# Splitting the next layer's weights earlier, a two-step low part, and tile addresses at multiples of 64 bytes

## The chip, the cores and the metric

The kernel runs on one NeuronCore of a Trainium2 chip. The metric is device time in microseconds (us) of the whole program; lower is better. TensorE (PE) multiplies, VectorE (DVE), ScalarE (ACT) and GpSimd (POOL) do elementwise work, SyncE (SP) issues all DMAs. Each engine works through its own instructions in order and waits for others by semaphores.

## The reference, cut to what matters

Two blocks of two layers each, on 512 tokens of width 1024 (and 256 context tokens in the first layer), all in float32:

```python
def reference(x, c, ctx, ...):
    x = first_block(x, c, ctx, ...)      # layer 0: window attention + short convolution; layer 1: HGRN2 scan
    return second_block(x, ...)          # an even and an odd mixer, each followed by a SwiGLU

def ab_layer(x, xc, mod, mod_c, w_in, w_out, ...):
    q, k, v, g_a, xb, b_g, c_g, g_b = split_cols(modulate(x, shift, scale) @ w_in, widths)
    ...
    y = jnp.concatenate([o_a * jax.nn.silu(g_a), o_b * jax.nn.silu(g_b)], axis=-1) @ w_out
    x_new = layer_norm(DEEPNORM_ALPHA * x + gate * y, ln_g, ln_b)

def second_block(x, ...):
    for layer in range(DEPTH):
        hn = rms_norm(x, norm_mix_pre[layer])
        mix = even_mixer(hn, ...) if layer % 2 == 0 else odd_mixer(hn, ...)
        x = x + rms_norm(mix, norm_mix_post[layer])
        hn = rms_norm(x, norm_ffn_pre[layer])
        ff = swiglu(hn, ffn_w_gate[layer], ffn_w_up[layer], ffn_w_down[layer])
        x = x + rms_norm(ff, norm_ffn_post[layer])
    return x
```

Every `@` here is a matrix product of the tokens with a weight matrix; those products are most of the work.

## The kernel before, in words

Activations stay transposed: a tile holds 128 features by up to 768 tokens, eight tiles make the width of 1024. A float32 product is made of three matmuls in the faster type fp32r: weights and inputs are each split into a high part (rounded to fp32r) and a low part (what the rounding left), and `product` (L293) adds high x high, high x low and low x high for each of eight tiles k. The names of a tile end in `_h` and `_l` for the two parts. In the profile's rows `mm<-act_h,wp_l` is a matmul into a bank of PSUM called mm, with the input tile act_h and the weight tile wp_l.

Weights come in blocks of 128 output columns, 512 KB each. `weights` (L269) loads a block into `wp_r` (3 buffers), rounds it to `wp_h` on ScalarE (`copy`, L243) and subtracts into `wp_l` (`sub`, L258) on VectorE, or on the engine given as `eng`. `wp_h` and `wp_l` have 4 buffers each, used in turn.

The stages run one after another: layer 0, layer 1, even, feed-forward 0, odd, feed-forward 1. A stage ends with `out_products` (L344): eight output blocks, the first ones over all tokens (512 columns per matmul), the last `keep` (3) by halves of 256 tokens (`PARTS`), so that the first half can be finished while the second is multiplied. These last blocks have their own buffers for `spare[1]` of them (pools w0, w5, w6, w7 or H). For each product `use` adds it to the running sums (res or po_mx or g_ff, and the sum of squares po_a or n_a). For each half `done` multiplies that sum with a matrix of ones (the matmul z, after which all partitions hold the mean), makes a reciprocal root, and then for each of the eight tiles k normalises, adds to the residual x and calls `emit` or `pre`, which write the next stage's inputs. `done` is a generator whose steps are interleaved with the second half's products.

`prenorm` (L1050) gives that `pre` for four boundaries (layer 1 to even, even to feed-forward 0, feed-forward 0 to odd, odd to feed-forward 1; the last stage has none): h is x times the norm's weight on ScalarE (`pn_h`), `act_h` its rounded copy on ScalarE, `act_l` the difference on GpSimd. `stats` then sums the squares of x into `res_acc`, and `rms` (L1079) turns it into the scale `res_rr` by a matmul with ones. At the boundary from layer 0 to layer 1 `emit` (L521) writes layer 1's inputs a_h and a_l, the subtraction in turns on VectorE and GpSimd.

The next stage begins with `firsts` (L304): three weight blocks, their low parts on GpSimd, are multiplied together tile by tile, first with the first half of the tokens, then with the second, so that each tile k is used as soon as it is there.

Three things set the order of work. Each engine's order is fixed when the program is built: a scheduler walks the instructions with priorities in the order in which the code emits them, and places one as soon as it reckons that it is ready. So a load or a split that the code emits late can still be placed early, where its buffers are free. The buffers' turns set the earliest time. And SP's order of DMAs is fixed in the same way.

Tiles lie in pools that are stacked from the left side of each partition's memory (const, wp, cond, a0, ...) or from the right (`side="right"`: a1, b2, b3, y1, z8, ...). A tile takes its width rounded up to 32 bytes.

Of the kernel before, what the change touches and what calls it, by code (L numbers as in the profile page):

```python
# [18 lines left out]
L = 512  # L19
# [169 lines left out]
class Prog:  # L189
    def __init__(self, es, tc, I, off):  # L190
# [21 lines left out]
        for v in (1e-5, 1e-6, np.pi / 2):  # L212
            t = self.const.tile([128, 1], F32, name=f"eps{int(v * 1e7)}")
            nc.gpsimd.memset(t, v)
            self.bias[v] = t
        self.rope2 = self.const.tile([128, 4], F32, name="rope2")
        nc.sync.dma_start(out=self.rope2, in_=I["rope2"])
        self.dummy = self.const.tile([128, 1], F32, name="dummy")

# [84 lines left out]
    def firsts(self, ps, blocks, xs, tags=("mm",) * 3):  # L304


        ws = [self.weights(b, eng=self.nc.gpsimd) for b in blocks]
        out = [ps(t) for t in tags]
        for s in PARTS[:2]:
            for k in range(KT):  # L310
                for p, w in zip(out[:3], ws):
                    self.product(p[:, s], w, xs, s, ks=(k,))
            for p, w in zip(out[3:], ws[3:]):
                self.product(p[:, s], w, xs, s)
        return list(zip(out, ws))
# [27 lines left out]

    def out_products(self, ps, block, xs, parts, use, done, keep=3, n=1024, late=(), begun=None, spare=(None, 0)):  # L344

# [19 lines left out]
        pool, own = spare  # L365
        ws = [self.weights(block(8 - keep + j), n, pool=pool if j < own else None) for j in range(keep)]
        last = iter(())
        for i, s in enumerate(parts):
# [27 lines left out]
    def conditioning(self, es):  # L396
# [12 lines left out]
        self.nc.vector.tensor_copy(out=self.sc[:, :, 0:2], in_=tv)  # L409
        self.sel = cond.tile([128, 2], F32, name="sel")  # L410
        self.nc.sync.dma_start(out=self.sel, in_=self.I["sel"])
# [41 lines left out]
    def layer0(self, stop=False):  # L453

        nc, tc = self.nc, self.tc
        with ExitStack() as es:
# [77 lines left out]
            use, done = self.deepnorm(N, ps, res, mod, emit)  # L534
            self.out_products(ps, lambda m: self.I["wo_ab"][m], xs2, PARTS, use, done, spare=(Alloc(es, tc, "w0", {"h": (1, 1024), "l": (1, 1024)}), 1))

# [281 lines left out]
    def layer1(self):  # L818
        nc, tc = self.nc, self.tc
        with ExitStack() as es:  # L820
# [23 lines left out]
            use, done = self.deepnorm(N, ps, self.x, self.mods[1], emit)  # L844
            self.out_products(ps, lambda m: self.I["wo_c"][m], xs2, PARTS[:2], use, done, spare=(Alloc(es, tc, "w5", {"h": (1, 1024), "l": (1, 1024)}), 1))
            for k in range(KT):
# [203 lines left out]
    def prenorm(self, es, ps, name, l):  # L1050


        nc = self.nc
        N = Alloc(es, self.tc, "pn", {"sq": (3, L), "h": (3, 256)})
        g = self.vec(name, 8 * l, 8 * l + 8)
        self.xs = [self.parts_of(self.A) for k in range(KT)]
        self.rr, self.acc = self.R("rr"), self.R("acc")

        def pre(k, s, x=None, scale=g, bias=None):
            hi, lo = self.xs[k]  # L1060
            h = N("h")
            x = self.x[k][:, s] if x is None else x
            if bias is None:
                self.act(h, x, ACT.Copy, scale=scale[:, k:k + 1])
            else:
                self.act(h, x, ACT.Identity, scale=scale[:, k:k + 1], bias=bias[:, k:k + 1])
            self.copy(hi[:, s], h)
            self.sub(lo[:, s], h, hi[:, s].bitcast(F32), nc.gpsimd)

        def stats():  # L1070
            for j in range(KT):
                sq = N("sq") if j else self.acc
                self.act(sq, self.x[j], ACT.Square)
                if j:
                    self.add(self.acc, self.acc, sq)

        return pre, stats
# [338 lines left out]
    def even(self):  # L1416
        tc = self.tc
        with ExitStack() as es:
# [5 lines left out]
            use, done = self.postnorm(es, ps, "norm_mix_post", 0, pre)  # L1424
            self.out_products(ps, lambda m: self.I["wo_ev"][m], xs2, PARTS[:2], use, done, late=(4, 5), begun=begun, spare=(Alloc(es, tc, "w6", {"h": (2, 1024), "l": (2, 1024)}), 2))
            stats()
# [212 lines left out]
    def odd(self):  # L1639
        tc = self.tc  # L1640
        with ExitStack() as es:
# [5 lines left out]
            use, done = self.postnorm(es, ps, "norm_mix_post", 1, pre)  # L1647
            self.out_products(ps, lambda m: self.I["wo_od"][m], xs2, PARTS[:2], use, done, late=(2, 4), spare=(Alloc(es, tc, "w7", {"h": (3, 1024), "l": (3, 1024)}), 3))
            stats()

    def odd_mix(self, es, B):
        nc, tc, xs, r = self.nc, self.tc, self.xs, self.rr
        A = Alloc(es, tc, "o7", {
            "sp2": (1, 8), "hb": (1, 16), "h": (4, L), "l": (4, L), "xb": (2, L + 3), "xc": (2, 1024),
            "tr": (2, 1024), "ti": (2, 1024), "a": (2, L), "mu": (2, L), "u": (2, 1024), "z": (2, 1024),
# [3 lines left out]
        sp = self.sp  # L1659
        sp2, hb = A("sp2"), A("hb")  # L1660
        self.ts(sp2, sp, 2.0, ALU.mult)
# [77 lines left out]
        halves, whole = (slice(0, L), slice(L, 2 * L)), (slice(0, 2 * L),)  # L1739
        first = dict(enumerate(self.firsts(ps, self.od[:3], xs)))  # L1740
        self.rms(ps("g"))
        cs, zs = {0: conv(0), 1: conv(1)}, {}
# [29 lines left out]
    def ffn(self, l, last=None):  # L1772

        nc, tc, xs, r = self.nc, self.tc, self.xs, self.rr
        with ExitStack() as es:
# [16 lines left out]
            for a, b in ((0, 6), (6, 14), (14, 22)):  # L1792
# [30 lines left out]
                else:  # L1823
# [4 lines left out]
                    use, done = self.postnorm(es, ps, "norm_ffn_post", l, pre, ff, last)  # L1828
                    self.out_products(ps, block, hs, PARTS[:2], use, done, n=n, keep=4 if last else 3, spare=(H, 2))
                    if stats:  # L1830
# [64 lines left out]
```

## Time and profile before

| | |
|---|---|
| three runs | 2106.44, 2109.29, 2116.51 us, median 2109.29 |
| profiled execution | 2109.53 us, of which the span is 2107.7 us |
| granted TensorE clock, mean | 0.986 of full speed |
| TensorE (matmuls) busy | 2038.4 us, 97% |
| VectorE, ScalarE, GpSimd busy | 1335.0, 918.5, 382.4 us |

Rows of the trace give a start in us from the span's start, a length, the engine, the line of the kernel, the operation, `output<-inputs`, the shape, and the number of instructions merged into the row; in brackets the idle time of the engine before it and what ended it. Matmuls overlap by their pipeline, so a matmul's own length (0.39 us) says less than the distance of two starts.

### The profile page before, as it was taken

How to read it: one execution, taken by the hardware profiler on the slowest of the kernel's cores; microseconds unless marked ns; L12 is line 12 of the kernel's file. 1: busy time of each engine (PE TensorE's matmuls, PEld its weight loads, DVE VectorE, ACT ScalarE, POOL GpSimd, SP SyncE). 2: the span in 40 equal slices, each digit the busy share in tenths (PEclk: the TensorE clock that was granted, in tenths of full speed). 3: DMA queues.
4: the chain of work that ended last, by engine and by line, in shares of the span. 5: the costliest groups of instructions: out<-in, count | busy, mean ns of one | idle time of the engine just before them, and what ended most of it. 6: DMA issues, size and time to landing. Idle time of an engine off the chain costs nothing. (4 is left out here: it accounts for less than half of the span.)

```text
span 2107.7 us, 30001 instructions
## 1 busy us (share of the span) xinstructions
PE 2038.4 (97%) x11624; PEld 1736.8 (82%) x11624; DVE 1335.0 (63%) x2302; ACT 918.5 (44%) x1642; POOL 382.4 (18%) x383
## 2 busy tenths in 40 slices
PE   6999999999999999989999999999989999999997
PEld 4888888889888888878778888888887888888886
DVE  6775566786666666787765764544567786344455
ACT  2564334445444444446566554322346654322231
POOL 1111111344222222033111420100020131010011
PEclk9999999999999999999999999999999999999998
DMA  8344442322111111224332398532325322333231
GB/s 307 117 155 138 148 137 73 116 82 77 42 52 57 53 51 41 90 96 146 115 100 81 132 325 321 170 100 91 121 98 201 130 90 88 103 100 100 91 109 41
DMA packets 91662, 246.91 MB, mean 117 GB/s; under 512 B 20480, under 2 KB 29440, under 8 KB 91520
## 3 DMA queue, kind: packets, MB, share of 16 engines
q1 hardware_dynamic: 91520, 245.01, 34.9%
q8 instruction: 91, 1.49, 0.3%
q14 instruction: 51, 0.42, 0.1%
HBM read 209.84 MB, written 35.13 MB: 116 GB/s over the span
## 5 line engine op out<-in xcount | busy, mean ns | idle before, releaser
L244 ACT ACTIVATE wp_h<-wp_r 128x1024 fp32r<-128x1024 f32 (+2 forms) x243 | 250.9, 1037 | 409.9 <-PE mm L318 245.8
L250 DVE TENSOR_TENSOR wp_l<-wp_r,wp_h 128x1024 fp32r<-128x1024 f32 (+1 forms) x228 | 319.6, 1404 | 100.2 <-ACT wp_h L244 100.1
L318 PE MATMUL mm<-act_l,wp_h 128*128 128x512 f32 (+1 forms) x1008 | 380.0, 377 | 2.6 <-POOL act_l L250 2.6
L318 PE MATMUL mm<-act_h,wp_h 128*128 128x512 f32 (+1 forms) x1008 | 377.5, 375 | 2.5 <-ACT act_h L244 2.5
L318 PE MATMUL mm<-act_h,wp_l 128*128 128x512 f32 (+1 forms) x1008 | 377.8, 375 | 0.0
L318 PE MATMUL mm<-a_h,wp_h 128*128 128x512 f32 (+1 forms) x920 | 337.1, 368 | 5.2 <-ACT wp_h L244 3.2
L318 PE MATMUL mm<-a_h,wp_l 128*128 128x512 f32 (+1 forms) x920 | 330.5, 360 | 0.4 <-POOL wp_l L250 0.4
L318 PE MATMUL mm<-a_l,wp_h 128*128 128x512 f32 (+1 forms) x920 | 329.3, 358 | 0.7 <-DVE a_l L250 0.6
L318 PEld LDWEIGHTS mm<-act_l,wp_h 128*128 128x128 f32 x1008 | 193.4, 192 | 36.4 <-POOL act_l L250 3.3
L318 PEld LDWEIGHTS mm<-act_h,wp_h 128*128 128x128 f32 x1008 | 192.3, 191 | 35.3 <-ACT act_h L244 2.9
L318 PEld LDWEIGHTS mm<-act_h,wp_l 128*128 128x128 f32 x1008 | 193.2, 192 | 33.0 <-issue 1.0
L318 PEld LDWEIGHTS mm<-a_h,wp_h 128*128 128x128 f32 x920 | 174.4, 190 | 30.2 <-issue 3.6
L318 PEld LDWEIGHTS mm<-a_l,wp_h 128*128 128x128 f32 x920 | 174.5, 190 | 25.9 <-issue 2.3
L318 PEld LDWEIGHTS mm<-a_h,wp_l 128*128 128x128 f32 x920 | 174.3, 189 | 24.0 <-issue 0.7
L250 POOL TENSOR_TENSOR g_g<-g_g,g_u 128x512 f32<-128x512 f32 x44 | 61.3, 1395 | 551.7 <-DVE g_u L250 510.0
L318 PE MATMUL mm<-h_l,wp_h 128*128 128x512 f32 (+1 forms) x344 | 129.2, 376 | 0.6 <-DVE h_l L250 0.5
L318 PE MATMUL mm<-h_h,wp_h 128*128 128x512 f32 (+1 forms) x344 | 129.0, 375 | 0.5 <-ACT h_h L244 0.5
L318 PE MATMUL mm<-h_h,wp_l 128*128 128x512 f32 (+1 forms) x344 | 128.8, 374 | 0.0
L250 DVE TENSOR_TENSOR g_u<-mm,res_rr 128x512 f32<-128x512 f32 x44 | 30.3, 689 | 110.6 <-PE mm L318 110.6
L244 ACT ACTIVATE m_km<-m_k 128x512 f32<-128x512 f32 x56 | 37.6, 672 | 122.9 <-DVE m_k L250 101.4
L247 ACT ACT_TABLE_LOAD x60 | 77.0, 1283 | 1.8 <-PEq L1883 0.7
L318 PEld LDWEIGHTS mm<-h_l,wp_h 128*128 128x128 f32 x344 | 64.8, 188 | 13.5 <-DVE h_l L250 2.1
(498 smaller groups left out, 3898.1 us busy)
## 6 DMA issues: line engine op xcount, KB each, us to landing
wp_r<-w_gu SPq DMA_DIRECT2D x88, 512.0 KB, 3.5
wp_r<-w_c SPq DMA_DIRECT2D x40, 512.0 KB, 3.5
wp_r<-wada SPq DMA_DIRECT2D x32, 512.0 KB, 3.7
wp_r<-w_d SPq DMA_DIRECT2D x32, 512.0 KB, 3.5
wp_r<-w_ab SPq DMA_DIRECT2D x26, 512.0 KB, 4.7
od_d<-z_h SPq DMA_DIRECT2D x20, 512.0 KB, 3.8
od_d<-z_l SPq DMA_DIRECT2D x20, 512.0 KB, 4.5
wp_h<-od_d SPq DMA_DIRECT2D x20, 512.0 KB, 3.3
```

Of the source, the lines that this page charges most:

```text
L244: self.nc.scalar.activation(out=out, in_=in_, func=ACT.Copy, scale=scale)
L247: self.nc.scalar.activation(out=out, in_=in_, func=func, **kw)
L250: (eng or self.nc.vector).tensor_tensor(out=out, in0=a, in1=b, op=op)
L318: self.nc.tensor.matmul(out=out, lhsT=a, rhs=b, start=start, stop=stop)
```

## The change

Four things:

- `out_products` takes a list `after` of the next stage's first weight blocks and splits up to `4 - keep + own` of them behind the split of its own last blocks and ahead of their products; `firsts` takes these (`self.ahead`) and splits only the rest. The early ones have their low part on VectorE, the default.
- `pre` without a bias writes the high part in one ScalarE operation, and the low part in one VectorE operation from x, the norm's weight and the high part. With a bias (layer 1 to even) it keeps its three steps, and the subtraction moves from GpSimd to VectorE.
- `sel`, `sp2` and `dummy` are allocated 16 columns wide (64 bytes), `rope2` in a pool of its own on the right side, at the very edge.
- In the odd layer the product of the fourth block stands ahead of `rms`.

```diff
@@ __init__
-        self.rope2 = self.const.tile([128, 4], F32, name="rope2")
+        self.edge = es.enter_context(tc.tile_pool(name="edge", bufs=1, side="right"))
+        self.rope2 = self.edge.tile([128, 4], F32, name="rope2")
...
-        self.dummy = self.const.tile([128, 1], F32, name="dummy")
+        self.ahead = []
+        self.dummy = self.const.tile([128, 16], F32, name="dummy")[:, 0:1]
@@ firsts
-        ws = [self.weights(b, eng=self.nc.gpsimd) for b in blocks]
+        ws = self.ahead + [self.weights(b, eng=self.nc.gpsimd) for b in blocks[len(self.ahead):]]
+        self.ahead = []
@@ out_products
         ws = [self.weights(block(8 - keep + j), n, pool=pool if j < own else None) for j in range(keep)]
+        self.ahead = [self.weights(b) for b in after[:4 - keep + own]]
@@ conditioning
-        self.sel = cond.tile([128, 2], F32, name="sel")
+        sel = cond.tile([128, 16], F32, name="sel")
+        self.sel = sel[:, 0:2]
@@ calls of out_products (own, after)
   layer0:  1, after=[self.I["w_c"][m] for m in range(3)]
   layer1:  1, after=[self.I["w_ev"][m] for m in (4, 8, 0)]
   even:    2, after=[self.I["w_gu0"][m] for m in range(3)]
   odd:     3, after=[self.I["w_gu1"][m] for m in range(3)]
   ffn:     2, after=() if last else self.od[:3]
@@ prenorm
         def pre(k, s, x=None, scale=g, bias=None):
-            hi, lo = self.xs[k]
-            h = N("h")
+            hi, lo = (t[:, s] for t in self.xs[k])
             x = self.x[k][:, s] if x is None else x
             if bias is None:
-                self.act(h, x, ACT.Copy, scale=scale[:, k:k + 1])
+                self.act(hi, x, ACT.Copy, scale=scale[:, k:k + 1])
+                self.stt(lo, x, scale[:, k:k + 1], hi.bitcast(F32), ALU.mult, ALU.subtract)
             else:
+                h = N("h")
                 self.act(h, x, ACT.Identity, scale=scale[:, k:k + 1], bias=bias[:, k:k + 1])
-            self.copy(hi[:, s], h)
-            self.sub(lo[:, s], h, hi[:, s].bitcast(F32), nc.gpsimd)
+                self.copy(hi, h)
+                self.sub(lo, h, hi.bitcast(F32))
@@ odd_mix
-            "sp2": (1, 8), "hb": (1, 16), ...
+            "sp2": (1, 16), "hb": (1, 16), ...
...
-        sp2, hb = A("sp2"), A("hb")
+        sp2, hb = A("sp2")[:, 0:8], A("hb")
...
         first = dict(enumerate(self.firsts(ps, self.od[:3], xs)))
+        first[3] = proj(3), None
         self.rms(ps("g"))
```

`self.od` holds the odd layer's weights already split: feed-forward 0 splits them in passing and stores both parts in DRAM (`odd_weights`, L1759), so `weights` only loads them.

## Rows read from the trace of the kernel before

**Rows 1.** The page's part 1, engines: busy us (share of the span) xinstructions.

```profile
PE 2038.4 (97%) x11624; PEld 1736.8 (82%) x11624; DVE 1335.0 (63%) x2302; ACT 918.5 (44%) x1642; POOL 382.4 (18%) x383
```

**Rows 2.** Waits of TensorE: who waited for whom, us in total, times, longest.

```profile
PE z L318 <- DVE po_a L250: 8.8, 4, 2.6
...
PE g L318 <- DVE res_acc L250: 3.1, 1, 3.1
...
PE mm L318 <- POOL act_l L250: 2.6, 3, 1.2
...
PE mm L318 <- POOL wp_l L250: 0.4, 1, 0.4
```

**Rows 3.** Windows at two boundaries: stretch, its us, busy us (instructions) by engine.

```profile
core 0: us, PE busy (x) PEld busy (x) DVE busy (x) ACT busy (x) POOL busy (x), PEclk, DMA share, GB/s
925.00:950.00 25.00, 19.80 (x148) 18.61 (x149) 22.39 (x52) 14.27 (x32) 12.00 (x12) 0.99 0.25 74
1175.00:1200.00 25.00, 20.00 (x154) 19.08 (x153) 22.86 (x45) 14.64 (x34) 11.81 (x11) 0.97 0.51 184
```

**Rows 4.** Timeline of TensorE, 512-column matmuls: first and next-after-last of three stretches.

```profile
1917.18 0.39 PE L318 MATMUL mm<-h_h,wp_h 128*128 128x512 f32 x1
...
1960.70 0.39 PE L318 MATMUL mm<-act_h,wp_h 128*128 128x512 f32 x1
...
1660.47 0.40 PE L318 MATMUL g<-o_h,wp_h 128*128 128x512 f32 x1
...
1666.09 0.40 PE L318 MATMUL mm<-act_h,wp_h 128*128 128x512 f32 x1
...
892.64 0.40 PE L318 MATMUL mm<-a_l,wp_h 128*128 128x512 f32 x1
...
901.31 0.39 PE L318 MATMUL mm<-a_h,wp_l 128*128 128x512 f32 x1
```

**Rows 5.** The same for 256-column matmuls, two stretches.

```profile
1563.95 0.27 PE L318 MATMUL mm<-act_h,wp_h 128*128 128x256 f32 x1
...
1577.62 0.39 PE L318 MATMUL mm<-act_h,wp_h 128*128 128x512 f32 x1
...
491.86 0.28 PE L318 MATMUL a<-a_h,wp_h 128*128 128x256 f32 x1
...
500.19 0.28 PE L318 MATMUL a<-a_h,wp_l 128*128 128x256 f32 x1
```

**Rows 6.** Groups of matmuls by form: xcount | busy us, mean ns | idle before.

```profile
L318 PE MATMUL mm<-a_h,wp_l 128*128 128x512 f32 x584 | 235.7, 404 | 0.0
...
L318 PE MATMUL mm<-a_h,wp_l 128*128 128x256 f32 x336 | 94.9, 282 | 0.4 <-POOL wp_l L250 0.4
...
L318 PE MATMUL mc<-a_h,wp_l 128*128 128x256 f32 x184 | 51.5, 280 | 0.0
...
L318 PE MATMUL mm<-b_l,wp_h 128*128 128x512 f32 x80 | 32.1, 401 | 0.3 <-DVE b_l L250 0.2
...
L318 PE MATMUL g<-o_l,wp_h 128*128 128x512 f32 x32 | 12.7, 396 | 0.0
```

**Rows 7.** Timeline of VectorE and of GpSimd at two boundaries.

```profile
1162.43 2.39 POOL L250 TENSOR_TENSOR wp_l<-wp_r,wp_h 128x1024 fp32r<-128x1024 f32 x1 [3.22 <-ACT wp_h L244]
...
1162.88 2.49 DVE L250 TENSOR_TENSOR po_a<-po_a,po_sq 128x512 f32<-128x512 f32 x1 [0.66 <-ACT po_sq L247]
...
1566.87 5.26 POOL L250 TENSOR_TENSOR act_l<-pn_h,act_h 128x256 fp32r<-128x256 f32 x5 [3.32 <-ACT act_h L244]
...
1567.26 0.75 DVE L250 TENSOR_TENSOR g_ff<-g_ff,po_r 128x256 f32<-128x256 f32 x2
...
1569.69 1.84 DVE L250 TENSOR_TENSOR g_ff<-g_ff,po_r 128x256 f32<-128x256 f32 x2
```

**Rows 8.** Groups of the low parts, and the odd layer's sum of squares in the timeline.

```profile
L250 POOL TENSOR_TENSOR act_l<-pn_h,act_h 128x256 fp32r<-128x256 f32 x64 | 57.4, 916 | 101.2 <-ACT act_h L244 100.9
...
L250 DVE TENSOR_TENSOR a_l<-n_h,a_h 128x256 fp32r<-128x256 f32 x12 | 5.1, 427 | 3.7 <-ACT a_h L244 3.5
...
1575.07 5.98 DVE L250 TENSOR_TENSOR res_acc<-res_acc,pn_sq 128x512 f32<-128x512 f32 x7 [1.55 <-ACT pn_sq L247]
```

More of the change, by code (lines that the diff above doesn't have):

```diff
@@ L342, in scores, with out_products @@
             self.matmul(out, q[h], k[:, cols], i == 0, i == 1)
-    def out_products(self, ps, block, xs, parts, use, done, keep=3, n=1024, late=(), begun=None, spare=(None, 0)):
+    def out_products(self, ps, block, xs, parts, use, done, keep=3, n=1024, late=(), begun=None, spare=(None, 0), after=()):
         wide = [X] + [s for s in parts if s.start >= L]
@@ L534, in layer0 @@
             use, done = self.deepnorm(N, ps, res, mod, emit)
-            self.out_products(ps, lambda m: self.I["wo_ab"][m], xs2, PARTS, use, done, spare=(Alloc(es, tc, "w0", {"h": (1, 1024), "l": (1, 1024)}), 1))
+            self.out_products(ps, lambda m: self.I["wo_ab"][m], xs2, PARTS, use, done, spare=(Alloc(es, tc, "w0", {"h": (1, 1024), "l": (1, 1024)}), 1), after=[self.I["w_c"][m] for m in range(3)])
     def layer0_mix(self, es, e0, late, xs, Y, first, s5):
@@ L844, in layer1 @@
             use, done = self.deepnorm(N, ps, self.x, self.mods[1], emit)
-            self.out_products(ps, lambda m: self.I["wo_c"][m], xs2, PARTS[:2], use, done, spare=(Alloc(es, tc, "w5", {"h": (1, 1024), "l": (1, 1024)}), 1))
+            self.out_products(ps, lambda m: self.I["wo_c"][m], xs2, PARTS[:2], use, done, spare=(Alloc(es, tc, "w5", {"h": (1, 1024), "l": (1, 1024)}), 1), after=[self.I["w_ev"][m] for m in (4, 8, 0)])
             for k in range(KT):
@@ L1424, in even @@
             use, done = self.postnorm(es, ps, "norm_mix_post", 0, pre)
-            self.out_products(ps, lambda m: self.I["wo_ev"][m], xs2, PARTS[:2], use, done, late=(4, 5), begun=begun, spare=(Alloc(es, tc, "w6", {"h": (2, 1024), "l": (2, 1024)}), 2))
+            self.out_products(ps, lambda m: self.I["wo_ev"][m], xs2, PARTS[:2], use, done, late=(4, 5), begun=begun, spare=(Alloc(es, tc, "w6", {"h": (2, 1024), "l": (2, 1024)}), 2), after=[self.I["w_gu0"][m] for m in range(3)])
             stats()
@@ L1647, in odd @@
             use, done = self.postnorm(es, ps, "norm_mix_post", 1, pre)
-            self.out_products(ps, lambda m: self.I["wo_od"][m], xs2, PARTS[:2], use, done, late=(2, 4), spare=(Alloc(es, tc, "w7", {"h": (3, 1024), "l": (3, 1024)}), 3))
+            self.out_products(ps, lambda m: self.I["wo_od"][m], xs2, PARTS[:2], use, done, late=(2, 4), spare=(Alloc(es, tc, "w7", {"h": (3, 1024), "l": (3, 1024)}), 3), after=[self.I["w_gu1"][m] for m in range(3)])
             stats()
@@ L1653, in odd_mix @@
         A = Alloc(es, tc, "o7", {
-            "sp2": (1, 8), "hb": (1, 16), "h": (4, L), "l": (4, L), "xb": (2, L + 3), "xc": (2, 1024),
+            "sp2": (1, 16), "hb": (1, 16), "h": (4, L), "l": (4, L), "xb": (2, L + 3), "xc": (2, 1024),
             "tr": (2, 1024), "ti": (2, 1024), "a": (2, L), "mu": (2, L), "u": (2, 1024), "z": (2, 1024),
@@ L1828, in ffn @@
                     use, done = self.postnorm(es, ps, "norm_ffn_post", l, pre, ff, last)
-                    self.out_products(ps, block, hs, PARTS[:2], use, done, n=n, keep=4 if last else 3, spare=(H, 2))
+                    self.out_products(ps, block, hs, PARTS[:2], use, done, n=n, keep=4 if last else 3, spare=(H, 2), after=() if last else self.od[:3])
                     if stats:
```

## The prediction, made before the result was known

> **What bounds the kernel now.** I read the busy shares first. TensorE runs for 2038.4 of 2107.7 us, and VectorE, the next, for 63% [rows 1]. So the time falls in two ways only: the matmuls get shorter, or some of the 69.3 us in which TensorE stands still go. The list of TensorE's waits says where those are: ones products that wait for a running sum (po_a: 8.8 us in four waits; res_acc: 3.1 us in one), low parts act_l from GpSimd (2.6 us in three), and almost nothing for a weight (0.4 us in one) [rows 2]. They lie at the layer boundaries: in 925 to 950 us TensorE works 19.80 of 25 us, in 1175 to 1200 us 20.00, and in both stretches VectorE is the fuller engine with 22.39 and 22.86 us [rows 3]. The boundaries are therefore VectorE's, not the weights'. Last I read matmul starts, since a busy TensorE hides how fast it goes.
>
> **Pools at multiples of 64 bytes.** A tile takes a multiple of 32 bytes of a partition. In the program before, `sel` (32 bytes) puts everything allocated after it up to layer 0's end at 32 past a multiple of 64, the inputs a_h and a_l among it; the top of the right-hand side also lies at 32 past one, and with it layer 1's a_h and a_l and the pools b; `sp2` does it to the odd layer's o_h and o_l. act_h, h_h and the weight pool wp begin at multiples of 64. The patch moves all of these onto multiples of 64: `sel`, `sp2` and `dummy` get 16 columns, rope2 goes to the right edge. Wide matmuls on inputs at 64: 192 starts from 1917.18 to 1960.70, 226.7 ns each. At 32: 24 of o from 1660.47 to 1666.09, 234.2 ns; 37 of a from 892.64 to 901.31, 234.3 ns [rows 4]. The o stretch lies between act matmuls of the same stage with the same weights pool, so neither stage nor load makes the difference. With 256 columns it is the other way round: 114 act matmuls from 1563.95 to 1577.62 are 119.9 ns apart, 71 of a from 491.86 to 500.19 only 117.3 ns [rows 5]. Counts: 512 columns 3 x 584 (a), 3 x 80 (b), 3 x 32 (o) = 2088; 256 columns 3 x 336 and 3 x 184 (a) = 1560 [rows 6]. If all go to the times at 64: 2088 x 7.6 ns = 15.9 us won, 1560 x 2.6 ns = 4.1 us lost, 11.8 us net. These stages keep TensorE full, so nearly all of it reaches the end; some of these matmuls wait for other engines anyway, and I take **-10 us**. Ends: -15.9 (no loss at 256) and +4.1 (no gain at 512).
>
> The Trainium skill's page "SBUF — State Buffer", section "Operand start alignment", asks only that an operand start at a multiple of its element size, 4 bytes here, and says that this is about legality and was not timed. The 7.6 ns of [rows 4] are thus something it does not know; by the page alone this part is worth nothing, which is rival A.
>
> **Low part of the inputs.** Before, a piece of 256 columns takes three steps: ScalarE writes h, ScalarE rounds it to act_h, GpSimd subtracts (64 times, 916 ns) [rows 8]. Now, at three of four boundaries (even to feed-forward 0, feed-forward 0 to odd, odd to feed-forward 1), ScalarE writes act_h directly and VectorE makes act_l in one operation; at layer 1 to even only the subtraction moves. VectorE gets 64 operations. Their nearest row is a_l on VectorE, 427 ns, so 27.3 us in all, 6.8 per boundary. Against it stands what GpSimd costs VectorE: two multiplications that take 0.75 us at 1567.26 take 1.84 at 1569.69, while GpSimd runs act_l from 1566.87 for 5.26 us [rows 7]. That is 0.54 us for each VectorE operation beside it, and if each of the 64 hits one, 35 us. So VectorE's load at a boundary stays about even, and what goes is GpSimd's own 916 ns at the end of each chain and the queue of act_l there.
>
> The Trainium skill's "SBUF — State Buffer", section "Who interferes with whom", calls the port pair of VectorE and GpSimd an exclusive lock held for a whole instruction. The sum at 1162.88, 2.49 us beside a GpSimd weight subtraction of 2.39 us [rows 7], agrees; by the rule alone a VectorE operation could lose up to the whole GpSimd one, 64 x 0.916 = 58.6 us, and the boundaries would gain more than I take.
>
> What it is worth is the idle at the boundaries that waits for act_l. Layer 1 to even and even to feed-forward 0 idle 5.2 and 5.0 us in their stretches [rows 3]. Of each I take 3 (**-6 us**), as the ones product's wait (8.8 / 4 = 2.2 us at the second kind [rows 2]) stays: the sum for it stands in VectorE's queue behind the first half's chain, in which 8 new operations are put. From odd to feed-forward 1 TensorE's wait is only that one: 0. Ends: both idles gone, -10.2 us; or no relief at all, and 8 x 0.427 = 3.4 us more in the first half's chain and 3.4 in the second's, 6.8 x 4 = +27.3 us. The new wait: VectorE's act_l waits for ScalarE's act_h, and behind it stand the next block's multiplications and the adds that the ones product needs.
>
> **Odd layer: the fourth product ahead of the mean square.** After the first products TensorE waits 3.1 us for res_acc [rows 2], whose seven adds end at 1575.07 + 5.98 = 1581.05 [rows 8]. The fourth product, 24 x 0.2267 = 5.4 us, now stands before it in order. TensorE is busy from 1577.62 [rows 5] to 1583.0, so the ones product comes up to 2.0 us later than it could, and with it the scaling and the gates behind it. Gain 3.1 - 2.0 = 1.1 us, up to 3.1 if the adds end earlier and the products behind fill in: **-1.5 us**. Ends: -3.1 and +2.0.
>
> **Weights split ahead.** At most 4 - 3 + own blocks come ahead: two at layer 0 to 1 and layer 1 to even, three elsewhere. But the order before has these splits ahead already: the subtraction for feed-forward 0 ran at 1162.43 [rows 7], more than 12 us ahead of the stretch in which that boundary idles [rows 3], and TensorE waited 0.4 us for weights' low parts in all [rows 2]. What is left is that VectorE does them: 2 + 2 + 3 + 3 = 10 subtractions leave GpSimd, and the weights from `od` were never split here. The third block at the first two boundaries stays on GpSimd, where it must wait for a buffer that the last products hold; the 0.4 us stay too. SP issues the same transfers. ScalarE's copy now stands before the squares of the last products; should it wait for a buffer, these wait with it. **0**, ends -0.4 and, for one ScalarE copy and subtraction more in front of the last sums, +1.2 at each of four boundaries (a 1024-wide subtraction as three of 427 ns, less overhead), +4.8.
>
> **Sum.** -10 - 6 - 1.5 + 0 = -17.5 us. The profiled execution took 2109.5 us, 1.8 of it around the span, and the median of the runs is 2109.29: the same within 0.01%. 2109.5 - 17.5 = **2092 us**.
>
> **The rivals.** *A, alignment is not the cause of the 7.6 ns*: what the slow inputs share could be their stage. For: layers 0 and 1 make up most of them. Against: o beside act in one stage. The boundaries' 7.5 us remain: 2102 us. *B, the boundaries give nothing*: VectorE is at 22.39 and 22.86 of 25 us [rows 3], takes 8 operations more per half, and the relief is used up by them; the wait only changes its name. For: the wait for po_a is VectorE's own. Against: 1.84 us for what takes 0.75. Alignment alone: 2099.5 us. *C, VectorE becomes the bound at the boundaries*: the VectorE operations stay long with GpSimd gone, or wait in order for act_h, and the whole 27.3 us lands on the path: 2109.5 + 27.3 - 10 = 2127 us. It is slower than before from the point where more than 10 + 1.5 of the 27.3 us, some 2.9 per boundary, are not given back. For: VectorE's order is fixed, so an early act_l blocks the add behind it. Against: 35 us against 27.3. *D, the splits don't come earlier*: forecast here at 0; were they a gain after all, 0.4 us.
>
> **How the numbers follow.** Forecast 0.66, A 0.13, B 0.13, C 0.08 (D lies in the forecast). A change under 0.5%, 10.5 us, can't be told from none: faster is under 2098.7, slower over 2119.8. Forecast gives nearly all to faster; B, at 2099.5, lies on the line and gives half; A gives little; C half slower. Faster 0.71, same 0.23, slower 0.06. The range for 8 in 10: down to 2081, where the 512-column gain comes whole without the loss and the boundaries give most of their idle; up to 2106, over A and B but short of C.
>
> **What would show it.** Alignment: a, b and o matmuls 227 ns apart, 256-column ones 120; if they keep 234 and 117, A. Low part: GpSimd has no act_l; VectorE's multiplications at the boundaries all near 0.4 us; TensorE's idle in the stretches that answer to 925 to 950 and 1175 to 1200 us near 2 us each; if these stay at 5 us, B, above 7, C. Fourth product: no wait of TensorE for res_acc, and a pause after the ones product in its place. Splits: GpSimd keeps 5 weight subtractions, the third block's at two boundaries and the three that the odd layer's output blocks have there. The prediction is wrong if the order of work elsewhere has changed so that a stage which now keeps TensorE full no longer does.

## The result and the profile after

The changed kernel takes 2088.8 us (median of 5 runs, 2085.4 to 2095.5) against 2106.7 us for the kernel before on the same chip: a ratio of 0.9909, 95% interval 0.9886 to 0.9933. The forecast was 2092.0 us. The total was nearly met; the terms under it were not. In the single edits the low part gave 14 us more than forecast, the alignment 7 less, and the fourth product cost 5 where it should have won 1.5.

The profiled execution of the changed kernel is the slowest of its five: 2095.5 us, span 2093.7 us, against 2109.5 and 2107.7 us before. Its page, part 1 (answers to [rows 1]):

```profile
PE 2033.3 (97%) x11624; PEld 1735.3 (83%) x11624; DVE 1325.0 (63%) x2376; ACT 903.6 (43%) x1594; POOL 302.2 (14%) x309
```

TensorE still bounds it. VectorE has 74 instructions more than before and is 10 us less busy; that is the first sign of where the time came from. TensorE's waits after the change (answers to [rows 2]; who waited for whom, us in total, times, longest):

```profile
PE mm L322 <- DVE o_xb L253: 3.8, 1, 3.8
...
PE mm L322 <- ACT act_h L250: 2.7, 1, 2.7
...
PE z L322 <- DVE po_a L253: 1.9, 1, 1.9
...
PE mm L322 <- DVE act_l L253: 1.2, 1, 1.2
...
PE mm L322 <- POOL wp_l L253: 1.1, 1, 1.1
...
PE s L322 <- DVE res_acc L253: 0.5, 1, 0.5
```

The ones products waited 8.8 us for po_a in four places before, now 1.9 us in one. The waits for act_l on GpSimd and for res_acc ahead of g are gone. New is the 3.8 us for o_xb in the odd layer, behind the ones product, where the prediction had looked for a pause.

Windows of 25 us at the four boundaries of `prenorm`, after the change (layer 1 to even, even to feed-forward 0, feed-forward 0 to odd, odd to feed-forward 1; the first two answer to [rows 3]):

```profile
core 0: us, PE busy (x) PEld busy (x) DVE busy (x) ACT busy (x) POOL busy (x), PEclk, DMA share, GB/s
921.00:946.00 25.00, 21.52 (x165) 20.55 (x165) 23.53 (x61) 16.49 (x37) 4.54 (x3) 1.00 0.31 95
1167.00:1192.00 25.00, 22.25 (x164) 21.49 (x163) 23.09 (x57) 12.99 (x26) 0.00 (x0) 0.91 0.51 188
1543.00:1568.00 25.00, 25.00 (x202) 24.53 (x201) 24.77 (x67) 13.06 (x28) 0.20 (x2) 1.00 0.14 46
1708.00:1733.00 25.00, 25.00 (x204) 24.53 (x203) 24.72 (x64) 12.81 (x27) 0.00 (x0) 1.00 0.01 2
```

The last one as it was before:

```profile
1718.00:1743.00 25.00, 22.39 (x163) 22.01 (x162) 22.12 (x43) 15.26 (x39) 13.24 (x16) 0.86 0.00 1
```

VectorE runs 64 instructions in these 25 us now where it ran 43, and GpSimd none. TensorE is full, and its granted clock is 1.00 instead of 0.86. In the first two windows TensorE still idles 3.5 and 2.8 us, where the prediction had named 2 as the sign of its gain and 5 as the sign of none.

To place the gain I matched the ones products, which both traces have in the same order. Starts, us:

```text
ones product                       before    after    after - before
layer 0, end (last z<-r_x)          404.01   402.69    -1.3
layer 1, end (last z<-res_x)        902.43   899.52    -2.9
even, beginning (last s<-res_acc)   985.06   976.97    -8.1
even, end (first z<-po_a)          1176.29  1168.15    -8.1
feed-forward 0 (second z<-res_acc) 1214.62  1208.46    -6.2
feed-forward 0, end                1547.90  1541.13    -6.8
odd, beginning (second g<-res_acc) 1582.11  1572.75    -9.4
odd, end                           1715.71  1706.49    -9.2
feed-forward 1                     1752.57  1738.11   -14.5
last ones product                  2096.05  2081.73   -14.3
```

Layers 0 and 1, where most of the alignment's 10 us should have come, gave 2.9. Three boundaries gave the rest: layer 1 to even 5.2, feed-forward 0 to odd 2.6, odd to feed-forward 1 5.2. Even to feed-forward 0 gave back 2; in five of the runs below whose edits lie elsewhere (e5, e6, e7, e11, e12) it is 1, the stretch being 39.1 us against 40.3 here and 38.3 before.

A second measure is used below, TensorE's *boundary loss*: in fixed stretches around the four boundaries (912 to 985, 1165 to 1265, 1535 to 1600, 1700 to 1765 us) it adds up by how much the distance of two starts exceeds 230 ns (512 columns) or 119 ns (256), wherever it is over 1.25 times that. It holds idle time and matmuls at the lower clock. Us:

```text
                       L1-even  even-f0  f0-odd  odd-f1   sum
before                   12.3      9.7    10.9     7.0   39.9
changed kernel            7.5     11.0     8.4     1.9   28.8
e2, low part alone        8.5      7.8     3.8     2.1   22.3
e3, fourth product alone 13.7     13.7    12.0     5.9   45.3
e4, weights ahead alone   9.8     13.8    11.4     5.9   40.9
e8, changed, no fourth    7.4     10.6     3.9     1.3   23.2
e9, subtraction moved     9.5      8.9     3.8     2.3   24.5
e10, GpSimd kept busy     8.7     14.5    11.9    10.1   45.1
e11, offsets              7.9      6.5     3.2     1.6   19.1
```

Executions of kernels that are the same at a place still differ there by up to 4 us (before and e3 at even to feed-forward 0), so only large differences of this table are read.

### The profile page after: what moved, and what is told of

It reads as the page before. It is cut to its first block, busy times and chain, and to the rows that moved or that the text cites. A ratio compares the mean times of both kernels' runs of the same rounds, so it can differ in the third digit from the quotient of the medians.

```text
span 2093.7 us, 29889 instructions
## 1 busy us (share of the span) xinstructions
PE 2033.3 (97%) x11624; PEld 1735.3 (83%) x11624; DVE 1325.0 (63%) x2376; ACT 903.6 (43%) x1594; POOL 302.2 (14%) x309
## 4 chain that ended last, share of the span: by engine, by line
PE 81%; DVE 10%; ACT 4%; issue 4%; DMA 1%; POOL 1%; SPq 0%; POOLq 0%; DVEq 0%; ACTq 0%
PE mm L322 61%; PE a L322 5%; PE mc L322 3%; PE x L322 2%; PE S L322 2%; PE s L322 1%; PE pt L663 1%; PE o L322 1%; PE mc L437 1%; PE z L322 1%; DVE r_x L253 1%; ACT L250 1%; DVE o_tr L253 1%; ACT wp_h L247 0%; DVE a_l L253 0%
## 5 line engine op out<-in xcount | busy, mean ns | idle before, releaser
L253 DVE TENSOR_TENSOR wp_l<-wp_r,wp_h 128x1024 fp32r<-128x1024 f32 (+1 forms) x238 | 323.9, 1362 | 102.3 <-ACT wp_h L247 102.3
L322 PEld LDWEIGHTS mm<-h_h,wp_h 128*128 128x128 f32 x344 | 65.1, 189 | 14.1 <-ACT h_h L247 2.3
```

The costliest lines, as they stand in the source:

```text
L253: (eng or self.nc.vector).tensor_tensor(out=out, in0=a, in1=b, op=op)
L322: self.nc.tensor.matmul(out=out, lhsT=a, rhs=b, start=start, stop=stop)
```

## The experiments

The experiments ran on several chips, each beside the kernel before on the same chip (medians 2106.8 to 2110.3 us there). The ratios are to that, so versions from different chips are compared by their ratios.

### One part at a time

**e1_align.** The kernel before, with these edits alone:

```diff
-        self.rope2 = self.const.tile([128, 4], F32, name="rope2")
+        self.edge = es.enter_context(tc.tile_pool(name="edge", bufs=1, side="right"))
+        self.rope2 = self.edge.tile([128, 4], F32, name="rope2")
...
-        self.dummy = self.const.tile([128, 1], F32, name="dummy")
+        self.dummy = self.const.tile([128, 16], F32, name="dummy")[:, 0:1]
...
-        self.sel = cond.tile([128, 2], F32, name="sel")
+        sel = cond.tile([128, 16], F32, name="sel")
+        self.sel = sel[:, 0:2]
...
-            "sp2": (1, 8), ...
+            "sp2": (1, 16), ...
...
-        sp2, hb = A("sp2"), A("hb")
+        sp2, hb = A("sp2")[:, 0:8], A("hb")
```

> The kernel before with the alignment edits alone (sel, sp2 and dummy 16 columns wide, rope2 in a pool at the right edge). Theory P, the prediction's: inputs at multiples of 64 bytes make the 512-column matmuls of a, b and o 226.7 ns apart and the 256-column ones 120 ns, -10 us, 2097 us. Theory A, its rival: a multiple of 64 is not what matters; the steady distances are those of the changed kernel (a 230.0 in layer 0 and 232.1 in layer 1, b about 233, o 233.3), layers 0 and 1 get 1.3 and 1.5 us shorter, b and o together under 0.5: -3 us, 2104 us, which times alone can hardly tell from no change.

Measured: 2106.9 us, ratio 0.9987 (0.9974 to 0.9999), some 2.7 us won. That is theory A; P's 10 us are excluded. All of a, b and o lie at multiples of 64, and their 512-column matmuls still start 230 to 231 (layer 0) and up to 233 ns (b and o) apart on average.

**e2_low.** The kernel before, with the new `pre` alone:

```diff
-                self.act(h, x, ACT.Copy, scale=scale[:, k:k + 1])
+                self.act(hi, x, ACT.Copy, scale=scale[:, k:k + 1])
+                self.stt(lo, x, scale[:, k:k + 1], hi.bitcast(F32), ALU.mult, ALU.subtract)
...
-            self.sub(lo[:, s], h, hi[:, s].bitcast(F32), nc.gpsimd)
+                self.sub(lo, h, hi.bitcast(F32))
```

> The kernel before with the new low part alone (ScalarE writes act_h directly, VectorE makes act_l). Theory P: -3 us at layer 1 to even, -3 at even to feed-forward 0, 0 at odd to feed-forward 1: -6 us, 2101 us. Theory Q, from the changed kernel's trace: about -5 us at layer 1 to even, 0 at even to feed-forward 0 and -5 at odd to feed-forward 1, if this edit is what took the 5 us there: -10 us, 2097 us. If odd to feed-forward 1 stays as before in this run, another edit (the weights split ahead) is what took them, and the sum is -5 us.

Measured: 2088.9 us, ratio 0.9904 (0.9888 to 0.9920). This edit alone makes the whole gain of the change. The boundary loss falls by 17.6 us: 3.8, 1.9, 7.1 and 4.9. Theory P is wrong by a factor of three, Q still too low. TensorE's wait for res_acc ahead of g is gone here too.

**e3_fourth** and **e4_ahead.** The kernel before with `first[3] = proj(3), None` ahead of `rms` alone, and with `self.ahead` and `after` alone.

> The kernel before with the odd layer's fourth product ahead of the mean square alone. Theory P: TensorE no longer waits for res_acc before the ones product, a pause comes behind it: -1.5 us (from -3.1 to +2.0), 2105 us. Rival: the pause behind is as long as the one taken away: 0.

> The kernel before with the next layer's weights split ahead of the last products alone. Theory P: 0 us (from -0.4 to +4.8), no boundary gets shorter. Rival R: ten weight subtractions off GpSimd free VectorE at the boundaries; odd to feed-forward 1 gets up to 5 us shorter and layer 1 to even up to 2: -5 to -7 us, 2100 to 2102 us.

Measured: 2108.7 us, ratio 0.9992 (0.9981 to 1.0004), and 2107.8 us, ratio 0.9991 (0.9980 to 1.0003). Neither differs from before. In e3 the wait for res_acc is gone and 3.7 us for o_xb stand in its place, as its rival said. Theory R for e4 is wrong at odd to feed-forward 1 (a loss of 5.9 us against 7.0); layer 1 to even is 2.5 us better, and even to feed-forward 0 is worse by the loss alone (the stretch between its ones products takes 38.5 us against 38.3).

### What in the low part makes the gain

**e9_subonly.** The kernel before with one argument less:

```diff
-            self.sub(lo[:, s], h, hi[:, s].bitcast(F32), nc.gpsimd)
+            self.sub(lo[:, s], h, hi[:, s].bitcast(F32))
```

> The kernel before with the subtraction for act_l moved from GpSimd to VectorE and nothing else: h is still written by ScalarE and rounded in a second ScalarE operation. Theory V (what counts is that GpSimd is out of the chain): most of the 19 us of the low part alone, -14 us or more, 2094 us or less; TensorE's idle plus half-clock loss at the four boundaries falls from 39.9 to about 25 us. Theory W (what counts is the ScalarE operation saved on every piece's way to act_h): less than half of it, 2099 us or more.

Measured: 2091.8 us, ratio 0.9928 (0.9909 to 0.9946), 15 us won. Theory V. The ScalarE operation saved would add 5 us on top by the two ratios, but the intervals of e9 and e2 overlap: that it adds anything is not shown.

**e10_beside.** e2_low, with GpSimd kept at work on something that nobody reads:

```diff
                 self.stt(lo, x, scale[:, k:k + 1], hi.bitcast(F32), ALU.mult, ALU.subtract)
+                self.sub(N("h"), x, hi.bitcast(F32), nc.gpsimd)
```

> The kernel before with the new low part, and beside it 64 GpSimd subtractions of the old kind (at the three boundaries without a bias 48 of them are issued) into a scratch tile that nobody reads: GpSimd is off the chain, but as busy as before. Theory X (GpSimd slows VectorE's operations beside it, by 0.54 us each): the four boundaries lose 10 us or more against the low part alone, 2099 to 2106 us. Theory Y (only act_l's way over GpSimd counted, 916 ns and its queue): no change against the low part alone, 2089 us.

Measured: 2113.6 us, ratio 1.0030 (1.0017 to 1.0044): slower than before, and 25 us slower than e2_low. Theory X, and more than it said. Groups of e10_beside (line, engine, operation, shape, count | busy us, mean ns | idle before):

```profile
L266 DVE SCALAR_TENSOR_TENSOR act_l<-res_x,vecs,act_h 128x256 fp32r<-128x256 f32 x48 | 35.6, 772 | 0.0
...
L266 DVE SCALAR_TENSOR_TENSOR res_x<-po_mx,vecs,res_x 128x256 f32<-128x256 f32 x32 | 18.6, 609 | 0.0
L266 DVE SCALAR_TENSOR_TENSOR res_x<-g_ff,vecs,res_x 128x256 f32<-128x256 f32 x32 | 18.6, 607 | 0.6 <-POOL g_ff L250 0.6
...
L250 POOL TENSOR_TENSOR pn_h<-res_x,act_h 128x256 f32<-128x256 f32 x48 | 44.2, 934 | 102.9 <-ACT act_h L247 102.6
```

The same groups of the changed kernel, where GpSimd is all but silent at the three boundaries:

```profile
L269 DVE SCALAR_TENSOR_TENSOR act_l<-res_x,vecs,act_h 128x256 fp32r<-128x256 f32 x48 | 21.3, 475 | 0.0
...
L269 DVE SCALAR_TENSOR_TENSOR res_x<-g_ff,vecs,res_x 128x256 f32<-128x256 f32 x32 | 16.2, 534 | 0.6 <-POOL g_ff L253 0.6
...
L269 DVE SCALAR_TENSOR_TENSOR res_x<-po_mx,vecs,res_x 128x256 f32<-128x256 f32 x32 | 14.3, 476 | 0.0
```

And of the kernel before:

```profile
L266 DVE SCALAR_TENSOR_TENSOR res_x<-po_mx,vecs,res_x 128x256 f32<-128x256 f32 x32 | 20.9, 678 | 0.0
L266 DVE SCALAR_TENSOR_TENSOR res_x<-g_ff,vecs,res_x 128x256 f32<-128x256 f32 x32 | 19.7, 640 | 0.6 <-POOL g_ff L250 0.6
```

The same VectorE operation takes 678 ns on average in the kernel before, with GpSimd at work beside it, and 476 ns in the changed one. Nobody waits for the extra results of e10. A rival would be that they hold up other work in GpSimd's queue; but VectorE and ScalarE wait for the same GpSimd tiles as in e2, each within 0.5 us, and TensorE for one weight's low part for 0.7 us against 0.4. The loss also lies where the theory puts it: 6.7, 8.1 and 8.0 us at the three boundaries with extra subtractions, and 0.2 us at layer 1 to even, which has none (e10 against e2 in the table above). What grew is TensorE's wait for VectorE's sum; first e2, then e10:

```profile
PE z L318 <- DVE po_a L250: 2.1, 2, 1.9
...
PE z L318 <- DVE po_a L250: 9.8, 5, 3.0
```

So most of the 25 us is the price of GpSimd working beside VectorE.

How that price reaches TensorE is seen at odd to feed-forward 1 in the kernel before (timeline of VectorE, GpSimd and TensorE: start, length):

```profile
1721.36 3.37 POOL L250 TENSOR_TENSOR act_l<-pn_h,act_h 128x256 fp32r<-128x256 f32 x4 [11.78 <-ACT act_h L244]
...
1721.41 0.42 DVE L1099 COPY po_mx<-mm 128x256 f32<-128x256 f32 x1
...
1723.17 0.96 DVE L250 TENSOR_TENSOR po_a<-po_a,po_sq 128x256 f32<-128x256 f32 x1
...
1727.41 0.94 DVE L250 TENSOR_TENSOR po_a<-po_a,po_sq 128x256 f32<-128x256 f32 x1
...
1728.40 0.80 PE L318 MATMUL z<-po_a,ones 128*128 128x256 f32 x1 [2.60 <-DVE po_a L250]
```

and in the changed kernel:

```profile
1717.43 0.41 DVE L253 TENSOR_TENSOR po_a<-po_a,po_sq 128x256 f32<-128x256 f32 x1
...
1717.90 0.70 PE L322 MATMUL z<-po_a,ones 128*128 128x256 f32 x2
```

The add to po_a takes 0.41 us instead of 0.94, the operations in the queue ahead of it are shorter too, and the ones product no longer waits. The difference is 0.53 us, less than the 0.84 us of one GpSimd subtraction in the first row (3.37 / 4). The Trainium skill's page "SBUF — State Buffer", section "Who interferes with whom", says that a VectorE operation with two inputs from SBUF contends with a GpSimd one that reads there, and that one with at most a single such input does not, outside the modes that use both of VectorE's ports. The trace agrees with both halves: the add to po_a, which reads two tiles in SBUF, takes 0.96 us at 1723.17, and the copy `po_mx<-mm`, which reads PSUM, 0.42 us at 1721.41, both within the 3.37 us of the first row.

### The fourth product

**e8_nofourth.** The changed kernel without it:

```diff
         first = dict(enumerate(self.firsts(ps, self.od[:3], xs)))
-        first[3] = proj(3), None
         self.rms(ps("g"))
```

> The changed kernel without the fourth product ahead of the mean square. Theory M: with the low part on VectorE the sum for the ones product is there early, so the fourth product in front of it only delays the scaling; idle plus half-clock loss of TensorE at feed-forward 0 to odd goes from 8.4 to about 3.8 us, as in the kernel before with the low part alone: -4.6 us, 2084 us. Rival N: it is the od weights ahead that cost there; then nothing changes, 2089 us. Theory P of the prediction: the fourth product is worth 1.5 us, so +1.5.

Measured: 2086.8 us, ratio 0.9889 (0.9872 to 0.9907) to the kernel before; the interval overlaps that of the changed kernel, so the times alone don't tell. The traces do: between the ones products at the end of feed-forward 0 and at the odd layer's end e8 gains 4.8 us on the changed kernel, and the boundary loss falls from 8.4 to 3.9 us: theory M. (Another 3.8 us of this execution lie in the even stage, where the clock from 1060 to 1140 us was 0.96 instead of 0.89; they are not the edit's.) Timeline of the changed kernel:

```profile
1567.06 3.08 DVE L253 TENSOR_TENSOR res_acc<-res_acc,pn_sq 128x512 f32<-128x512 f32 x4
...
1572.33 1.02 PE L322 MATMUL g<-res_acc,ones 128*128 128x512 f32 x2
1577.10 0.80 PE L322 MATMUL mm<-act_h,wp_h 128*128 128x512 f32 x1 [3.75 <-DVE o_xb L253]
1577.69 0.63 PE L322 MATMUL mm<-act_l,wp_h 128*128 128x512 f32 x1
1578.12 0.63 PE L322 MATMUL mm<-act_h,wp_l 128*128 128x512 f32 x1
```

and of e8:

```profile
1565.51 1.12 PE L322 MATMUL g<-res_acc,ones 128*128 128x512 f32 x2
...
1570.38 0.50 PE L322 MATMUL mm<-act_h,wp_h 128*128 128x512 f32 x1 [1.45 <-DVE o_xb L253]
1570.72 0.40 PE L322 MATMUL mm<-act_l,wp_h 128*128 128x512 f32 x1
1570.96 0.39 PE L322 MATMUL mm<-act_h,wp_l 128*128 128x512 f32 x1
```

In the changed kernel the sum is complete at 1570.14 (1567.06 + 3.08), but the ones product stands behind the fourth product until 1572.33, and the scaling with all that hangs on it comes later by as much. TensorE then idles 3.75 us, and after that its matmuls start 0.43 us apart until 1583.2: the lower clock, 1.2 GHz. In e8 the fourth product stands behind the ones product and fills that time, the wait is 1.45 us, and the matmuls behind it run 0.23 us apart. Windows of 30 us, the changed kernel and then e8:

```profile
1566.00:1596.00 30.00, 26.25 (x107) 20.85 (x106) 21.11 (x35) 16.65 (x24) 0.41 (x4) 0.89 0.55 205
```

```profile
1560.00:1590.00 30.00, 28.55 (x131) 22.78 (x130) 24.22 (x42) 19.08 (x29) 0.40 (x4) 1.00 0.64 231
```

### What sets the pitch of the matmuls

If it is not the multiple of 64, something else sets the pitch (the distance of two starts) of 226.7 against 234 ns. The addresses of the tiles in the built programs show a candidate: wp_h and wp_l, act and h all begin 320 bytes past a multiple of 512. In the changed kernel a of layer 0 lies 64 bytes past that, a of layer 1 and b 128, o 192.

**e5_same512.** The changed kernel, a, b and o moved to the weights' offset:

```diff
-        sel = cond.tile([128, 16], F32, name="sel")
+        sel = self.edge.tile([128, 32], F32, name="sel")
...
-            "sp2": (1, 16), ...
+            "sp2": (1, 96), ...
```

> The changed kernel with three tiles resized, so that the inputs of every product (a, b, o) begin at the same offset within 512 bytes as the weights wp; act and h already do. Theory S (the distance between moving and stationary addresses within 512 bytes sets the pitch): all 512-column matmuls 226.7 to 227 ns apart (from 230.0 in layer 0, 232.1 in layer 1, 233 for b and o), all 256-column ones 119.8 to 120: about 700 x 3.2 + 1050 x 5.3 + 240 x 6 + 96 x 6.5 = 9.9 us won, 800 x 3.2 + 800 x 1.2 = 3.5 lost, -6 us, 2083 us. Theory 64 (a multiple of 64 is what matters): they are at multiples of 64 already, no change, 2089 us. Theory L (the layer, not the address): no change, 2089 us.

**e6_shift64.** The changed kernel, act, h and o moved by 64 bytes, the weights in wp not:

```diff
-        self.A = Alloc(self.es, self.tc, "act", {"h": (8, L), "l": (8, L)})
+        self.A = Alloc(self.es, self.tc, "act", {"pad": (1, 16), "h": (8, L), "l": (8, L)})
+        self.nc.gpsimd.memset(self.A("pad"), 0.0)
```

> The changed kernel with 64 bytes put in front of act, so that act, h and o move by 64 bytes and the weights wp stay. Theory S: act and h fall to the pitch of layer 0's a, which is 64 bytes off: about 230 ns with 512 columns and 117 with 256; some 3500 x 3.3 = 11.5 us lost, some 700 x 2.8 = 2 won, +9 us, 2098 us. Theory 64: still multiples of 64, no change, 2089 us. Theory L: no change.

**e7_all64.** The changed kernel, weights and the left side moved together, the right side not:

```diff
-        self.dummy = self.const.tile([128, 16], F32, name="dummy")[:, 0:1]
+        self.dummy = self.const.tile([128, 32], F32, name="dummy")[:, 0:1]
```

> The changed kernel with 64 bytes put in front of the weights and everything on the left behind them, so that wp, a of layer 0, act, h and o move together, and only the right-hand side (a of layer 1, b) stays: it is now 64 instead of 128 bytes off the weights. Theory S: act and h keep 226.7 and 120, a of layer 0 keeps 230.0 and 116.7, a of layer 1 goes from 232.1 to about 230: some 1050 x 2 = 2 us won, 2087 us. Theory O (the input's own address within 512 bytes counts, whatever the weights'): act and h go to 230 as in the kernel with act alone shifted, +9 us, 2098 us.

Measured: 2091.0, 2093.3 and 2087.9 us; ratios to the kernel before 0.9904 (0.9888 to 0.9920), 0.9914 (0.9897 to 0.9931) and 0.9886 (0.9869 to 0.9902). The intervals overlap that of the changed kernel; the pitches speak. In each fence the first row begins a stretch of equal matmuls and the second is the one behind it.

o, 24 matmuls, in the changed kernel (192 bytes off): 5.60 / 24 = 233.3 ns, and in e5 (0 off): 5.44 / 24 = 226.7 ns.

```profile
1607.45 0.39 PE L322 MATMUL g<-o_h,wp_h 128*128 128x512 f32 x1
...
1613.05 0.39 PE L322 MATMUL mm<-act_h,wp_h 128*128 128x512 f32 x1
```

```profile
1604.94 0.39 PE L322 MATMUL g<-o_h,wp_h 128*128 128x512 f32 x1
...
1610.38 0.39 PE L322 MATMUL mm<-act_h,wp_h 128*128 128x512 f32 x1
```

act in feed-forward 1, 384 matmuls, in e6 (64 off): 87.90 / 384 = 228.9 ns, and in e7 (0 off, both moved): 87.04 / 384 = 226.7 ns, as in [rows 4].

```profile
1813.82 0.39 PE L322 MATMUL mm<-act_h,wp_h 128*128 128x512 f32 x1
...
1901.72 0.39 PE L322 MATMUL mm<-h_h,wp_h 128*128 128x512 f32 x1
```

```profile
1808.81 0.39 PE L322 MATMUL mm<-act_h,wp_h 128*128 128x512 f32 x1
...
1895.85 0.39 PE L322 MATMUL mm<-h_h,wp_h 128*128 128x512 f32 x1
```

b, 72 matmuls, in the changed kernel (128 off): 16.80 / 72 = 233.3 ns, and in e7 (64 off): 16.49 / 72 = 229.0 ns.

```profile
1141.56 0.39 PE L322 MATMUL mm<-b_h,wp_h 128*128 128x512 f32 x1
...
1158.36 0.28 PE L322 MATMUL mm<-b_h,w_h 128*128 128x256 f32 x1
```

```profile
1139.54 0.40 PE L322 MATMUL mm<-b_h,wp_h 128*128 128x512 f32 x1
...
1156.03 0.28 PE L322 MATMUL mm<-b_h,w_h 128*128 128x256 f32 x1
```

The same stretch of the same stage changes with nothing but the distance of the two operands' addresses: theory S. Theory 64, theory L and theory O (e7 moved act's own address and kept its pitch) are out. Times moved less than S said. In e6 the pitch rose by 2.2 ns where S had 3.3. In e5 layer 0 and 1 mix 512- and 256-column matmuls, where the mean with 512 columns is about 230 ns at 0 as well as at 64 bytes, while the 256-column ones went from about 117 and 118.7 to 119.5 and 119.6: my sum had used the pitch of pure stretches for mixed ones.

**e11_offsets.** The changed kernel with what the runs pointed to:

```diff
-        self.rope2 = self.edge.tile([128, 4], F32, name="rope2")
+        self.rope2 = self.edge.tile([128, 24], F32, name="rope2")[:, 0:4]
...
-            "sp2": (1, 16), ...
+            "sp2": (1, 96), ...
...
-        first[3] = proj(3), None
```

> The changed kernel without the fourth product ahead, o at the weights' offset within 512 bytes, and layer 1's a and b 64 bytes off it instead of 128. From the runs so far: the fourth product out, -4.8; layer 1's a from 232.1 to 229.8 ns with 512 columns and 118.7 to 117.8 with 256, -3; o 6.5 ns x 96 and b 3 ns x 240, -1.3: -9 us against the changed kernel, 2080 us. If the executions' own spread of the clock hides it: 2086 us, as without the fourth product.

Measured: 2080.9 us, ratio 0.9876 (0.9853 to 0.9900). It is the fastest version of this study, 26 us under the kernel before and 7 by the ratios under the changed one (whose interval its own just overlaps). In its trace the span is 13.3 us shorter than the changed kernel's: layer 1 (from the last z<-n_a of layer 0 to the last z<-res_x) gives 4.5, the odd layer with its beginning 5.1. Of the other 3.7 us, 2.8 lie in feed-forward 0, where its edits change nothing.

**e12_off256.** e11 with layer 1's a 256 bytes off:

```diff
-            self.a1 = Alloc(self.es1, tc, "a1", {"h": (8, LT), "l": (8, LT)}, side="right")
+            self.a1 = Alloc(self.es1, tc, "a1", {"h": (8, LT), "l": (8, LT), "pad": (1, 80)}, side="right")
...
+            nc.gpsimd.memset(self.a1("pad"), 0.0)
```

> The same as the kernel with offsets, but layer 1's a 256 bytes off the weights' offset instead of 64 (80 columns put above it in its pool). Theory S says that the distance of the addresses sets the pitch, not which way it goes at 256: in the kernel with act shifted, o lay 256 bytes off and took 227.9 ns with 512 columns, 1.9 less than a at 64 bytes; with 256 columns unknown, between 113.3 (h at 64) and 120 (0). So layer 1 between 2 us shorter and 2 us longer than in the kernel with offsets. If the address within 512 bytes does not count in layer 1: no change.

Measured: 2083.1 us, ratio 0.9884 (0.9864 to 0.9905), the same as e11 within the intervals. Layer 1 takes 3.0 us more than in e11, past the range given: its 256-column matmuls go from about 116 to about 119 ns, the 512-column ones stay at about 230. A distance of 256 bytes thus looks like 0 (119.6 and 230 in e5).

## Why the prediction was right, and where it was wrong

**The total** was forecast at 2092.0 and came out at 2088.8, inside the range. It is right by luck: the low part's error of 14 us is cancelled by the alignment's 7 and the fourth product's 6, which only the single edits show. These do account for the change: -19.5 (e2), -2.7 (e1), +4.8 (the fourth product, by e8) and 0 (e4) make -17.4 us, and 17.9 were measured.

**Low part, forecast -6, measured -19.5** (e2). The failed step is that "the ones product's wait" "stays" at the first two boundaries, and with it "From odd to feed-forward 1 TensorE's wait is only that one: 0". I had the price of GpSimd beside VectorE (0.54 us for each operation) and used it only to say that VectorE's load stays even. But VectorE's queue is what the ones products wait for, and it got faster by that very price: the waits for po_a went from 8.8 to 1.9 us, and at odd to feed-forward 1, where I forecast nothing, 5 us went. At feed-forward 0 to odd, for which the low part's term had nothing at all, it took 7 (e2). The wait for res_acc went by this edit too, without any reordering: e2 keeps the old order, and TensorE's list of waits has none at g.

**Even to feed-forward 0** gave less than the 3 us: 1.9 of boundary loss in e2, which is within the scatter there, and nothing in the changed kernel. What is late there is a third thing, for which the prediction had not looked: weight splits for the odd layer stand between the steps of the reciprocal root in VectorE's order. They stood there before the change as well, at 1190.25 and 1192.56 us. In the changed kernel:

```profile
1182.82 0.41 DVE L269 SCALAR_TENSOR_TENSOR po_t<-z,po_r 128x256 f32<-128x256 f32 x1
1183.15 1.21 DVE L253 TENSOR_TENSOR z_l<-z_r,z_h 128x1024 fp32r<-128x1024 f32 x1
1184.28 0.41 DVE L269 SCALAR_TENSOR_TENSOR po_t<-po_t,po_r 128x256 f32<-128x256 f32 x1
1184.62 1.21 DVE L253 TENSOR_TENSOR z_l<-z_r,z_h 128x1024 fp32r<-128x1024 f32 x1
1185.75 0.41 DVE L269 SCALAR_TENSOR_TENSOR po_r<-po_t,po_r 128x256 f32<-128x256 f32 x1
```

The root thus takes 3.3 us (1182.82 to 1186.16), 2.4 of it splits, and by the order in the trace TensorE's 2.7 us for act_h follow from it (it starts again at 1187.95). No run moved these splits, so this is read from the trace and not shown.

**Alignment, forecast -10, measured -2.7** (e1). The failed step is that a multiple of 64 makes the 7.6 ns. Rival A was right on this term, though not for its reason: it is the address, but its distance from the weights'. I had compared act at 64 with o at 32 and called the difference alignment; between them the distance to the weights differed as well. The check that the prediction itself named decided it: a, b and o did not come to 227 ns.

**Fourth product, forecast -1.5.** Alone it is worth nothing (e3), and beside the new low part it costs 4.8 us in the trace (e8; the intervals of the times overlap). The prediction had the mechanism (the ones product comes later than it could) and its price of 2.0 us, but took the 3.1 us as won by this edit; the low part had removed them already. The 3.75 us of idle that follow cost twice, since behind them the matmuls start 0.43 us apart instead of 0.23.

**Weights ahead, forecast 0, measured 0** (e4), with 5 weight subtractions left on GpSimd, as said.

**Rivals B and C.** The boundaries give most of the gain, so B is out. C's mechanism did not decide: VectorE's 64 new operations (21.3 + 8.2 us) are paid for by the time that the others no longer lose, and VectorE is less busy than before.

## What to carry to other kernels

When two engines slow each other, take the gain of freeing one not only at the wait that names it but along the whole queue of the other, down to everything that waits for that queue. Test each edit of a bundle alone: here one of four made the gain, and one cost 5 us only beside it. And before a difference in pitch is put down to one property of an address, list the others that differ with it.

## What the runs showed of the hardware that was not expected

The pitch of back-to-back fp32r matmuls depends on the distance of the moving from the stationary operand's address. In pure stretches of 512 columns: 226.7 to 227.8 ns at 0 bytes, 233.3 at 32, 228.8 to 229.1 at 64, 232.3 (a) and 233.3 (b) at 128, 234.0 to 234.3 at 160, 233.3 at 192, 227.2 to 228.8 (o in e6) at 256. With 256 columns it is 120 ns at 0 and 256 bytes. At 64 bytes two values occur, even for one tile: in e7 the 48 matmuls of layer 1's a from 908.6 us are 117.9 ns apart, the 48 from 918.0 us 113.3 ns; h came down to 113.3 ns in e6. Why is open, and so is whether the distance counts within 512 or within 256 bytes.
